# A two-layer decoder trunk on one core: sliding pooling sums rewritten as band-matrix products over tokens

## The chip, the core and the metric

The kernel runs on one core of one Trainium2 chip. The metric is the device time of one execution in microseconds (us). The core has a matrix engine (PE; its weight loads are listed apart as PEld), three engines that work on elements (DVE, ACT, POOL), and a queue engine (SP) that issues most transfers; transfers can also be issued from the queues of ACT and POOL. On-chip memory has 128 partitions; products land in eight accumulation banks of 128 x 512 values (PSUM).

## The reference, cut to what matters

The input x has 512 tokens of 1024 values. Two layers follow: layer 0 mixes tokens with a multi-scale causal pooling mixer, layer 1 with attention; after each mixer comes a SwiGLU feed-forward block (FFN), and a norm ends the trunk. The change concerns only the pooling mixer of layer 0:

```python
POOL_WINDOWS = (2, 4, 8, 16)          # one window for each group of 256 channels

def pool_mixer(h, w_in, w_group, scale, w_out):
    B, S, _ = h.shape
    u = jnp.einsum('bsd,de->bse', h, w_in).reshape(B, S, N_POOL_GROUPS, POOL_GROUP_DIM)
    cs = jnp.cumsum(u.astype(jnp.float32), axis=1)
    pos = jnp.arange(S)
    outs = []
    for g, w in enumerate(POOL_WINDOWS):
        c = cs[:, :, g]
        lag = jnp.pad(c, ((0, 0), (w, 0), (0, 0)))[:, :S]
        cnt = jnp.minimum(pos + 1, w).astype(jnp.float32)[None, :, None]
        outs.append((c - lag) / cnt - u[:, :, g].astype(jnp.float32))
    p = jnp.stack(outs, axis=2).astype(h.dtype)
    z = jnp.einsum('bsgc,gce->bsge', p, w_group).reshape(B, S, D_MODEL) * scale
    return jnp.einsum('bsd,de->bse', z, w_out)

h = rmsnorm(x, norm_mix[0]); x = x + pool_mixer(h, ...)
```

So there are three products, the input product (1024 x 1024), the group product (four times 256 x 256) and the output product (1024 x 1024), and between the first two each token's value is replaced by the mean of the last w tokens minus the value itself.

## The kernel before

**Layout.** Channels lie on partitions in eight chunks of 128 (`NC = 8`), tokens along the free side, in the order `TOKENS`: residue modulo 4 outermost (`R = 4`), 128 tokens for each residue (`J = 128`). A product of one chunk of inputs with one chunk of outputs is done in near-full precision: each operand is split into a high part and a remainder (`hi`, `lo`), and `mm3` (line 193) issues three products, of 512 columns each. A step with 8 chunks on both sides is 8 x 8 x 3 = 192 such products.

**Weights.** They are listed in use order in `queue`. `weights(i)` (line 101) loads up to five items ahead into the raw tiles of pool `wraw` (five buffers, line 63) and splits up to four ahead into pool `wspl` (three buffers, line 64): a cast on ACT makes `whi` (line 118), a subtraction on DVE makes `wlo` (line 119). All these loads are issued from SP, in order.

**What sets the order.** PE's order is written out by the program (`manual_schedule`, line 68). For the other engines the framework picks the order, one stream per engine, and a waiting instruction holds back whatever stands behind it on its engine.

**The pooling mixer before the change.** `j_two` (line 130) loads weights for outputs 0 and 1 in pieces, between the loads of x (line 334). `split_scaled` (line 312) makes `h_hi` and `h_lo` from x with the norm's gain; the squares (line 344) are added on DVE and POOL (line 347) into `norm.ssq` and `other`, and these two are added (line 348). PE starts on the input product at once: outputs 0 and 1 into two of the banks `early0` to `early3` while inputs arrive; `project` (line 198) does the others. The token norm is applied to the result: inside output 2, PE sums the squares for each token (`token_sums`, line 264, four small products), DVE and ACT take the inverse root, make four diagonal matrices (`diagonals`, line 275), and PE spreads them to all partitions (`spread`, line 285), copied to `rB`. Then for each of the eight output chunks e, in the order 6, 7, 4, 5, 2, 3, 0, 1 (line 368): `u` = result x `rB` on DVE (line 382); one to four doubling steps `winsum` on POOL and DVE (lines 391, 393, 396); `p` = sum/w - u (line 401); a correction of the first tokens (lines 406, 407); and the split into `p_hi` (ACT, line 326) and `p_lo` (POOL, line 327).

Only after all eight input products PE does the group products, in two halves of 24 products (line 410), the first on groups 3 and 2. Their results are scaled and split into `z_hi` and `z_lo` (lines 422, 423). Then come the eight output products (line 428), each followed by `residual` (line 320), which adds to x, splits for the FFN and squares for its norm. In these stages `weights` hands out `j_grp[0]`, `j_grp[1]`, `j_out[0]` to `j_out[7]`, in that order.

Of the kernel before, what the change touches and what calls it, by code (L numbers as in the profile page):

```python
# [17 lines left out]
P = 128  # L18
# [14 lines left out]
PAD = 8  # L33
# [18 lines left out]
def trunk_kernel(ctx: ExitStack, tc: tile.TileContext, xT, gam, consts, ident_d, w0, w1, wv, w_down, outT):  # L52
# [19 lines left out]

    queue = []
# [3 lines left out]
    SPLITS = {"w": 3, "v": 2}  # L77
    RAWS = {"w": 5, "v": 2}

    def enqueue(src, shape):  # L80
        queue.append(dict(kind="w", src=[src], shape=shape))
        return len(queue) - 1
# [18 lines left out]
    def weights(i, split_ahead=4, load_ahead=5):  # L101
        if "ahead" in queue[i]:
            load_ahead = queue[i]["ahead"]
        while len(raws) < min(len(queue), i + load_ahead):
            raws.append(load(queue[len(raws)]))
        while len(ready) < min(len(raws), i + split_ahead):
            item = queue[len(ready)]
            kind, shape = item["kind"], item["shape"]
            if len(ready) > i and live(ready, i, kind) == SPLITS[kind]:
                break  # L110
            n = math.prod(shape)
            raw = raws[len(ready)]
            if "plus" in item:
                nc.vector.tensor_add(raw[:, :n], raw[:, :n], raws[item["plus"]][:, :n])  # L114
            pool = pools["v"] if kind == "v" else wspl
            hi = pool.tile([P, 1024], F32R, name=kind + "hi")
            lo = pool.tile([P, 1024], F32R, name=kind + "lo")
            nc.scalar.copy(hi[:, :n], raw[:, :n])  # L118
            nc.vector.tensor_sub(lo[:, :n], raw[:, :n], hi[:, :n].bitcast(F32))  # L119
# [9 lines left out]
    PIECES = ((0, 2), (2, 2), (4, 4))  # L129
    j_two = [[enqueue(w0[i][:, s * P : (s + n) * P], (n, P)) for i in range(2)] for s, n in PIECES]  # L130
    j_in = [None, None] + [enqueue(w0[i], (8, P)) for i in range(2, 8)]
    j_grp = [enqueue(w0[8 + i], (4, 2 * P)) for i in range(2)]
    j_out = [enqueue(w0[10 + i], (8, P)) for i in range(8)]

# [58 lines left out]
    def mm3(ps, whi, wlo, xhi, xlo, first, last):  # L193
        nc.tensor.matmul(ps, lhsT=whi, rhs=xhi, start=first, stop=False)  # L194
        nc.tensor.matmul(ps, lhsT=whi, rhs=xlo, start=False, stop=False)  # L195
        nc.tensor.matmul(ps, lhsT=wlo, rhs=xhi, start=False, stop=last)  # L196
# [95 lines left out]
    class InverseRms:  # L292
# [5 lines left out]
        def columns(self):  # L298
# [4 lines left out]
            self.diag = diagonals(self.r, 4)  # L303
# [26 lines left out]
    first = []  # L330
    for (at, n), js in zip(PIECES, j_two):
        for i, w in enumerate(js):
            for c in range(at + i * n // 2, at + (i + 1) * n // 2):
                nc.sync.dma_start(x[:, c, :], xT[c * P : (c + 1) * P, :])
            first.append((at, n, i, weights(w, 1, 1)))
    nc.scalar.dma_start(ident, ident_d)
    for c in range(NC):
        split_scaled(c, 0)

    norm = Norm()  # L340
    other = tmp.tile([P, S], F32, name="rB")
    for c in range(NC):
        sq = norm.ssq if c == 0 else other if c == 1 else tmp.tile([P, S], F32, name="sq", bufs=2)
        nc.scalar.activation(sq, x[:, c, :], AF.Square)
        if c > 1:
            acc, eng = (other, nc.gpsimd) if c % 2 else (norm.ssq, nc.vector)
            eng.tensor_add(acc, acc, sq)
    nc.vector.tensor_add(norm.ssq, norm.ssq, other)

    KS = list(range(NC))  # L350
    with ExitStack() as pctx:
        pm = pctx.enter_context(tc.tile_pool(name="poolmix", bufs=1, reuse_waits="tile"))
        pw = pctx.enter_context(tc.tile_pool(name="poolw", bufs=3, reuse_waits="tile"))
        pmm = pctx.enter_context(tc.tile_pool(name="pmm", bufs=1, space=bass.MemoryType.PSUM))
        p_hi = pm.tile([P, NC, S], F32R, name="p_hi")
        p_lo = pm.tile([P, NC, S], F32R, name="p_lo")
        z_hi = pm.tile([P, NC, S], F32R, name="z_hi")
        z_lo = pm.tile([P, NC, S], F32R, name="z_lo")
        invc = pm.tile([P, 4 * R * HEAD], F32, name="invc")
        nc.scalar.dma_start(invc, consts[:, 0 : 4 * R * HEAD])  # L360
        order = [6, 7, 4, 5, 2, 3, 0, 1]


        early = [pmm.tile([P, S], F32, name=f"early{i}") for i in range(4)]
        for at, n, i, (whi, wlo) in first:
            for c in range(at, at + n):
                mm3(early[i], whi[:, c - at, :], wlo[:, c - at, :], h_hi[:, c, :], h_lo[:, c, :], c == 0, c == NC - 1)
        for n, e in enumerate(order):
            g = e // 2
            ps = early[n] if n < 4 else None  # L370
            if n == 0:
                inv_rms = InverseRms(norm.parts)
                project([j_in[2]], h_hi, h_lo, KS, early[2], {3: inv_rms.columns})
                inv_rms.rows()
                rB = inv_rms.rB
                project([j_in[3]], h_hi, h_lo, KS, early[3])
            elif n > 3:
                ps = project([j_in[n]], h_hi, h_lo, KS, ps)
            u = pw.tile([P, R, PAD + J], F32, name="u")
            nc.gpsimd.memset(u[:, :, :PAD], 0.0)  # L380
            rows = lambda t: t.rearrange("p (r j) -> p r j", r=R)
            nc.vector.tensor_mul(u[:, :, PAD:], rows(ps), rows(rB))
            s = u
            at = 0
            for lev in range(g + 1):
                sh = 1 << lev
                t = pw.tile([P, R, PAD + J], F32, name="winsum")
                eng = nc.gpsimd if lev < g - 1 or (lev == 0 and g) else nc.vector

                if sh < R:  # L390
                    eng.tensor_add(t[:, sh:, at:], s[:, sh:, at:], s[:, : R - sh, at:])
                    at += 1
                    eng.tensor_add(t[:, :sh, at:], s[:, :sh, at:], s[:, R - sh :, at - 1 : -1])
                else:
                    back = sh // R
                    eng.tensor_add(t[:, :, at + back :], s[:, :, at + back :], s[:, :, at:-back])
                    at += back
                s = t
            w = WINDOWS[g]
            p = pw.tile([P, S], F32, name="p")  # L400
            nc.vector.scalar_tensor_tensor(rows(p), s[:, :, PAD:], 1.0 / w, u[:, :, PAD:], op0=ALU.mult, op1=ALU.subtract)

            n_head = max(w // R, 1)
            hd = pw.tile([P, R, HEAD], F32, name="head")
            inv = invc[:, g * R * HEAD : (g + 1) * R * HEAD].rearrange("p (r j) -> p r j", r=R)
            nc.vector.tensor_mul(hd[:, :, :n_head], s[:, :, PAD : PAD + n_head], inv[:, :, :n_head])
            nc.vector.tensor_sub(rows(p)[:, :, :n_head], hd[:, :, :n_head], u[:, :, PAD : PAD + n_head])
            split(p_hi[:, e, :], p_lo[:, e, :], p, nc.gpsimd)
        zs = []
        for half in range(2):  # L410
            whi, wlo = weights(j_grp[half])
            for gg in range(2):
                g = 3 - (2 * half + gg)
                for m in range(2):
                    e = 2 * g + m
                    ps = early[2 * gg + m] if half == 0 else mm.tile([P, S], F32, name="mm")
# [320 lines left out]
    with ExitStack() as actx:  # L737
# [9 lines left out]
        at = 4 * R * HEAD  # L747
# [311 lines left out]
def _constants():  # L1059
    first = R * np.arange(HEAD)[None, :] + np.arange(R)[:, None]  # L1060
    inv = np.stack([np.float32(1.0) / np.minimum(first + 1, w).astype(np.float32) for w in WINDOWS])
# [13 lines left out]
    parts = [np.tile(inv.reshape(1, -1), (P, 1)), cos, sin, near, prev, near, own, comb]  # L1075
# [9 lines left out]
def _layout(x, norm_mix, norm_ffn, norm_final, pool_w_in, pool_w_group, pool_scale, pool_w_out,  # L1085
# [3 lines left out]
    w_in = _tiles(pool_w_in[0], 8)[[6, 7, 4, 5, 2, 3, 0, 1]]  # L1089
# [10 lines left out]
        xT=x[0].T[:, TOKENS], gam=gam, consts=_constants(), ident=np.eye(P, dtype=np.float32),  # L1100
# [18 lines left out]
```

## Time and profile before

| | us |
|---|---|
| median of the runs (1036.52 to 1040.21) | 1036.99 |
| the profiled execution | 1036.61 |
| its span on the core | 1034.8 |
| PE busy | 1011.8 (98% of the span) |
| DVE busy | 802.2 (78%) |
| ACT busy | 517.8 (50%) |
| POOL busy | 189.5 (18%) |
| transfers read from device memory | 140.96 MB, 138 GB/s over the span |

Times inside the profile are counted from the start of the span. A view in rows of time gives for each entry its start, its length, the engine, the line of the kernel, the operation and the tiles it writes and reads; in square brackets stands how long the engine was idle before it and what ended that. Products are pipelined in PE: a row's length includes the pipeline, so the pace is read from the distance of two starts. A product of type float32 shows as two records, the split ones (fp32r) as one. A view by stretches gives for each engine the busy time and the number of instructions in a stretch, then the granted clock of PE (1.00 is full), and the share and rate of transfers.

### The profile page before, as it was taken

The page shows a single profiled execution, that of the slowest core. Times are in us where ns is not written, and L with a number is a line of the kernel's source. Part 1 is how long each engine was busy: PE and PEld are TensorE (multiplying, and loading weights), DVE is VectorE, ACT ScalarE, POOL GpSimd, SP SyncE. Part 2 cuts the span into 40 slices and gives each one's busy share as a digit, 9 for nine tenths or more (in the row PEclk, how much of TensorE's full clock was granted, in tenths as well). Part 3 has the DMA queues.
Part 4 walks back from the last instruction along what each step waited for, and adds up shares of the span by engine and source line. Part 5 has one row for each costly group of instructions (what it writes and reads, how often), then busy time and mean ns, then how long its engine had stood idle before and what let it go on. Part 6 is the DMA issues. An engine that isn't in the chain of part 4 may idle for free.

```text
span 1034.8 us, 17396 instructions
## 1 busy us (share of the span) xinstructions
PE 1011.8 (98%) x6986; PEld 934.4 (90%) x6986; DVE 802.2 (78%) x1100; ACT 517.8 (50%) x797; POOL 189.5 (18%) x163
## 2 busy tenths in 40 slices
PE   8979999999999999999999999999999999999996
PEld 6758888999999999988777899888999999999996
DVE  6894489898888888677888636559989789788844
ACT  6243446554655555452534433444664555465444
POOL 1742300111111111022333300210011110101003
PEclk9989999999999999999999999999999999999998
DMA  7132445667668767432212143424568766966702
GB/s 271 59 102 89 141 121 135 152 194 202 163 168 233 187 139 191 141 115 82 82 45 76 52 132 94 134 82 123 123 157 216 209 149 176 230 155 163 183 29 82
DMA packets 75201, 144.19 MB, mean 139 GB/s; under 512 B 6384, under 2 KB 30576, under 8 KB 75120
## 3 DMA queue, kind: packets, MB, share of 16 engines
q1 hardware_dynamic: 56992, 113.33, 34.0%
q0 software_dynamic: 16320, 28.32, 16.9%
q10 hardware_dynamic: 1808, 1.43, 0.4%
q8 instruction: 54, 0.88, 0.3%
q14 instruction: 27, 0.22, 0.1%
HBM read 140.96 MB, written 2.10 MB: 138 GB/s over the span
## 4 chain that ended last, share of the span: by engine, by line
PE 84%; DVE 9%; issue 2%; DMA 2%; POOL 1%; ACT 1%; SPq 0%; ACTq 0%; DVEq 0%; POOLq 0%
PE p L567 29%; PE r L567 15%; PE mm L194 8%; PE mm L195 8%; PE mm L196 8%; PE mm L567 7%; DVE wlo L119 2%; PE mm L269 1%; PE mm L1008 1%; PE mm L1007 1%; PE mm L1009 1%; PE early L194 1%; PE tp L874 1%; PE early L195 1%; PE early L196 1%
## 5 line engine op out<-in xcount | busy, mean ns | idle before, releaser
L118 ACT CAST whi<-wraw 128x1024 fp32r<-128x1024 f32 (+4 forms) x201 | 194.3, 968 | 254.1 <-PE p L567 103.8
L119 DVE TENSOR_TENSOR wlo<-wraw,whi 128x1024 fp32r<-128x1024 f32 (+4 forms) x201 | 231.7, 1153 | 38.4 <-ACT whi L118 37.6
L119 DVE TENSOR_TENSOR vlo<-vraw,vhi 128x1024 fp32r<-128x1024 f32 (+1 forms) x90 | 100.3, 1116 | 42.9 <-ACT vhi L118 41.7
L118 ACT CAST vhi<-vraw 128x1024 fp32r<-128x1024 f32 (+1 forms) x90 | 86.7, 965 | 80.8 <-PE r L567 55.0
L196 PE MATMUL mm<-h_hi,wlo 128*128 128x512 f32 x312 | 121.8, 390 | 2.8 <-DVE wlo L119 2.8
L194 PE MATMUL mm<-h_hi,whi 128*128 128x512 f32 x312 | 123.7, 397 | 0.0
L195 PE MATMUL mm<-h_lo,whi 128*128 128x512 f32 x312 | 121.5, 389 | 0.0
L567 PE MATMUL p<-t_hi,whi 128*128 128x256 f32 x288 | 81.2, 282 | 0.1
L567 PE MATMUL p<-t_lo,whi 128*128 128x256 f32 x288 | 81.1, 282 | 0.0
L567 PE MATMUL r<-h_hi,vhi 128*128 128x256 f32 x288 | 81.1, 281 | 0.0
L567 PE MATMUL p<-t_hi,wlo 128*128 128x256 f32 x288 | 81.0, 281 | 0.0
L567 PE MATMUL r<-h_hi,vlo 128*128 128x256 f32 x288 | 81.0, 281 | 0.0
L567 PE MATMUL r<-h_lo,vhi 128*128 128x256 f32 x288 | 80.9, 281 | 0.0
L196 PEld LDWEIGHTS mm<-h_hi,wlo 128*128 128x128 f32 x312 | 58.6, 188 | 15.7 <-DVE wlo L119 3.2
L194 PEld LDWEIGHTS mm<-h_hi,whi 128*128 128x128 f32 x312 | 58.6, 188 | 14.1 <-issue 1.7
L195 PEld LDWEIGHTS mm<-h_lo,whi 128*128 128x128 f32 x312 | 58.6, 188 | 11.6
L114 DVE TENSOR_TENSOR vraw<-vraw,wraw 128x1024 f32<-128x1024 f32 (+1 forms) x60 | 66.9, 1115 | 0.6
L567 PE MATMUL p<-u_hi,whi 128*128 128x256 f32 x216 | 61.1, 283 | 0.0
L567 PE MATMUL p<-u_hi,wlo 128*128 128x256 f32 x216 | 61.1, 283 | 0.0
L567 PE MATMUL p<-u_lo,whi 128*128 128x256 f32 x216 | 61.0, 282 | 0.0
L98 POOL DMA_DIRECT2D wraw<-w x18 | 21.8, 1208 | 210.5 <-DVE ct L517 47.9
L250 POOL TENSOR_TENSOR ssq<-ssq,sq 128x512 f32<-128x512 f32 x20 | 32.1, 1607 | 141.7 <-issue 77.0
(278 smaller groups left out, 3004.5 us busy)
## 6 DMA issues: line engine op xcount, KB each, us to landing
wraw<-w SPq DMA_DIRECT2D x131, 512.0 KB, 3.8
wraw<-w_down SPq DMA_DIRECT2D x48, 384.0 KB, 3.3
vraw<-w SPq DMA_DIRECT2D x18, 512.0 KB, 6.1
vraw<-w POOLq DMA_DIRECT2D x18, 512.0 KB, 6.8
wraw<-w POOLq DMA_DIRECT2D x18, 512.0 KB, 7.5
vraw<-w_down SPq DMA_DIRECT2D x12, 384.0 KB, 4.1
vraw<-w_down POOLq DMA_DIRECT2D x12, 384.0 KB, 5.7
wraw<-w_down POOLq DMA_DIRECT2D x12, 384.0 KB, 6.8
```

The lines of the kernel that those rows point to most:

```text
L98: nc.gpsimd.dma_start(dst, more, accum_op=ALU.add)
L114: nc.vector.tensor_add(raw[:, :n], raw[:, :n], raws[item["plus"]][:, :n])
L118: nc.scalar.copy(hi[:, :n], raw[:, :n])
L119: nc.vector.tensor_sub(lo[:, :n], raw[:, :n], hi[:, :n].bitcast(F32))
L194: nc.tensor.matmul(ps, lhsT=whi, rhs=xhi, start=first, stop=False)
L195: nc.tensor.matmul(ps, lhsT=whi, rhs=xlo, start=False, stop=False)
L196: nc.tensor.matmul(ps, lhsT=wlo, rhs=xhi, start=False, stop=last)
L250: nc.gpsimd.tensor_add(self.ssq, self.ssq, sq)
L269: nc.tensor.matmul(cols[:, i : i + 1], lhsT=sq[:, b * P : (b + 1) * P], rhs=ones[:, :1], start=j == 0, stop=j == len(parts) - 1,)
L567: nc.tensor.matmul(ps[:, g, :], lhsT=w[:, g, c, :], rhs=xx, start=i in (0, 1, 3) and g + c + k == 0, stop=c == n - 1 and k == 2, skip_grou ...
L874: nc.tensor.transpose(tp[:, j, :], todo[i + j], ident)
L1007: nc.tensor.matmul(o, lhsT=xh, rhs=whi[:, kk, :], start=kc == 0, stop=False)
```

## The change

The tokens are put on partitions for the first half of the mixer. The roles in the input product are swapped: `h` blocks of 128 tokens are the stationary side, the weights the moving side, so a result holds 128 tokens x 512 channels. For this x is loaded in natural token order (`xN`), and a second time in the order `TOKENS` (`xT`) for the residual. The norm is then a factor for each partition, applied when a result is read out (`u_out`). The window means become products with a constant band matrix over tokens (`windows`): for each block of 128 tokens and each chunk of 128 channels, the block's `u_hi` and `u_lo` are stationary, and the band, 4 x 36 columns (the block's own tokens and up to 16 after it, for each residue), is moving; the result has channels on partitions again. Block 0 has counts below w in its band, and a third product of 16 columns for the remainder of its values. `p` is split from the bank directly (ACT and DVE).

The order on PE is new as well: first half of the input product, `token_sums` with two parts, blocks 0 and 1 of the second half, `windows(0)`, block 2, part of `windows(1)`, block 3, first group products, the rest of `windows(1)`, the known half of outputs 0 and 1, second group products, the known half of output 2, and then the output products. The second half's weights have a pool of their own (`poolb`, four buffers); when it closes, `z_hi` and `z_lo` take its place.

```diff
-    SPLITS = {"w": 3, "v": 2}
+    SPLITS = {"w": 3, "v": 2, "b": 4}
...
+    j_in = [[enqueue(w0[0][:, i * S : (i + 1) * S], (1, S)) for i in range(2)] + [enqueue(w0[i], (2, S)) for i in range(1, 4)]]
+    j_in.append([enqueue(w0[i], (2, S), "b") for i in range(4, 8)])
+    j_grp, j_out = [enqueue(w0[8], (4, 2 * P))], [enqueue(w0[10 + i], (8, P)) for i in range(2)]
+    j_grp.append(enqueue(w0[9], (4, 2 * P)))
+    j_out += [enqueue(w0[10 + i], (8, P)) for i in range(2, 8)]
...
+        held = ExitStack()
+        pools["b"] = held.enter_context(tc.tile_pool(name="poolb", bufs=4, reuse_waits="tile"))
+        early = [pmm.tile([P, S], F32, name=f"early{i}") for i in range(4)]
...
+        for c in range(NC):
+            if c < 2 or c % 2 == 0:
+                at = c if c < 2 else 1 + c // 2
+                load_x = lambda cc: nc.sync.dma_start(x[:, cc, :], xN[cc * P : (cc + 1) * P, :])
+                if c < 2:
+                    load_x(c)
+                whi, wlo = weights(j_in[0][at], 1, 1)
+                if c >= 2:
+                    load_x(c)
+                    load_x(c + 1)
+            for b in range(4):
+                blk = slice(b * P, (b + 1) * P)
+                k = 0 if c < 2 else c % 2
+                if b == 0:
+                    split_scaled(c, 0)
+                mm3(early[b], h_hi[:, c, blk], h_lo[:, c, blk], whi[:, k, :], wlo[:, k, :], c == 0, c == NC - 1)
...
+        w_second = [weights(j) for j in j_in[1]]
+        nc.sync.dma_start(bands.rearrange("p g k r j -> p (g k r j)"), consts[:, 0 : 8 * R * SPAN])
+        nc.sync.dma_start(ident, ident_d)
+        nc.scalar.copy(bands_hi, bands)
...
+        for c in range(NC):
+            nc.sync.dma_start(x[:, c, :], xT[c * P : (c + 1) * P, :])
+        inv_rms = InverseRms([norm.ssq, other])
+        inv_rms.columns(diag=False)
+
+        def u_out(b, half, ps):
+            nc.scalar.activation(u_hi[:, b, half, :], ps, AF.Copy, scale=inv_rms.r[:, b : b + 1])
+            nc.vector.scalar_tensor_tensor(
+                u_lo[:, b, half, :], ps, inv_rms.r[:, b : b + 1], u_hi[:, b, half, :].bitcast(F32),
+                op0=ALU.mult, op1=ALU.subtract,
+            )
...
+        def windows(half, blocks):
+            for i in range(4):
+                e = 4 * (1 - half) + i
+                out = early[i].rearrange("p (r j) -> p r j", r=R)
+                for b in blocks:
+                    n = min(SPAN, J - 32 * b)
+                    band = bands_hi[:, e // 2, min(b, 1), :, :n]
...
+                    mat(to, u_hi, band, start=b == 0, stop=False)
+                    mat(to, u_lo, band, start=False, stop=b == 3)
+                    if b == 0:
+                        mat(out[:, :, :HEAD], u_hi, bands_lo[:, e // 2, :, :], start=False, stop=False)
+                if blocks[-1] == 3:
+                    split(p_hi[:, e, :], p_lo[:, e, :], early[i])
...
+        for b in range(4):
+            u_out(b, 0, early[b])
+        second(0)
+        second(1)
+        windows(0, range(4))
+        second(2)
+        windows(1, range(2))
+        second(3)
+        held.close()
...
+        group_products(0, None)
+        windows(1, range(2, 4))
...
+        known, rest = [6, 7, 4, 5], [2, 3, 0, 1]
...
+        for m in range(2):
+            out_part(m, known)
+        group_products(1, early)
+        out_part(2, known)
         for m in range(NC):
-            residual(m, project([j_out[m]], z_hi, z_lo, order, early[m] if m < 4 else None), 1, norm)
+            if m > 2:
+                out_part(m, known)
+            residual(m, out_part(m, rest), 1, norm)
```

`second(b)` is the input product of token block b with the second 512 channels, 24 products into a bank of pool `mm` and then `u_out`. `out_part(m, cs)` fetches `weights(j_out[m])` at its first call and adds the chunks `cs` of output m; it keeps the split weights until its last call. The pooling loop with `winsum`, `head` and `rB`, the tiles `invc` and `u`, and the first call of `diagonals` and `spread` are gone.

More of the change, by code (lines that the diff above doesn't have):

```diff
@@ L327, in split @@
         (eng or nc.vector).tensor_sub(lo, src, hi.bitcast(F32))
[L330 to L348, printed above, removed]
     KS = list(range(NC))
     with ExitStack() as pctx:
[L352 to L354 removed]
+        open_pool = lambda name, bufs, **kw: pctx.enter_context(tc.tile_pool(name=name, bufs=bufs, reuse_waits="tile", **kw))
@@ L359, in trunk_kernel @@
[L359 to L408, printed above, removed]
@@ L409, in trunk_kernel @@
-        zs = []
-        for half in range(2):
+        u_hi = pm.tile([P, 4, 2, S], F32R, name="u_hi")
+        u_lo = pm.tile([P, 4, 2, S], F32R, name="u_lo")
+        bands = pm.tile([P, 4, 2, R, SPAN], F32, name="bands")
+        bands_hi = pm.tile([P, 4, 2, R, SPAN], F32R, name="bands_hi")
+        bands_lo = pm.tile([P, 4, R, HEAD], F32R, name="bands_lo")
+        norm = Norm()
+        other = tmp.tile([P, S], F32, name="rB")
+        for c in range(NC):
[14 more added lines that the diff above has]
+                mm3(early[b], h_hi[:, c, blk], h_lo[:, c, blk], whi[:, k, :], wlo[:, k, :], c == 0, c == NC - 1)
+            sq = norm.ssq if c == 0 else other if c == 1 else tmp.tile([P, S], F32, name="sq", bufs=2)
+            nc.scalar.activation(sq, x[:, c, :], AF.Square)
+            if c > 1:
+                acc, eng = (other, nc.gpsimd) if c % 2 else (norm.ssq, nc.vector)
+                eng.tensor_add(acc, acc, sq)
@@ new lines, in u_out, with second @@
+        def u_out(b, half, ps):
[4 more added lines that the diff above has]
+            )
+        def second(b):
+            blk = slice(b * P, (b + 1) * P)
+            ps = mm.tile([P, S], F32, name="mm")
+            for c in range(NC):
+                whi, wlo = w_second[c // 2]
+                mm3(ps, h_hi[:, c, blk], h_lo[:, c, blk], whi[:, c % 2, :], wlo[:, c % 2, :], c == 0, c == NC - 1)
+            u_out(b, 1, ps)
@@ L415, in trunk_kernel @@
                     e = 2 * g + m
-                    ps = early[2 * gg + m] if half == 0 else mm.tile([P, S], F32, name="mm")
+                    ps = banks[2 * gg + m] if banks else mm.tile([P, S], F32, name="mm")
                     for k in range(2):
@@ L1059, in _constants @@
 def _constants():
-    first = R * np.arange(HEAD)[None, :] + np.arange(R)[:, None]
-    inv = np.stack([np.float32(1.0) / np.minimum(first + 1, w).astype(np.float32) for w in WINDOWS])
+    s, d = np.arange(P)[:, None], (np.arange(R)[:, None] + R * np.arange(SPAN)[None, :]).reshape(1, -1)
+    bands = []
+    for w in WINDOWS:
+        inside = (s <= d) & (s > d - w)
+        for count in (np.minimum(d + 1, w), w):
+            bands.append(np.where(inside, np.float32(1.0) / np.float32(count), np.float32(0.0)) - (s == d).astype(np.float32))
     freq = (np.float32(1.0) / np.float32(10000.0) ** (np.arange(0, HD, 2, dtype=np.float32) / np.float32(HD))).astype(np.float32)
@@ L1074, in _constants @@
     comb = np.where((k <= q) & (k % 4 == q % 4), 0.0, NEG)
-    parts = [np.tile(inv.reshape(1, -1), (P, 1)), cos, sin, near, prev, near, own, comb]
+    parts = bands + [cos, sin, near, prev, near, own, comb]
     return np.ascontiguousarray(np.concatenate(parts, 1).astype(np.float32))
```

47 lines of the change are left out of this document (29 added, 18 removed).

## The prediction

> **What bounds the kernel now.** I read the page first: PE is busy nearly all the time, so only what PE waits for, or runs slowly, can be won.
>
> ```profile
> PE 1011.8 (98%) x6986; PEld 934.4 (90%) x6986; DVE 802.2 (78%) x1100; ACT 517.8 (50%) x797; POOL 189.5 (18%) x163
> ```
>
> Then the view by stretches, cut where PE's work changes: inputs arrive and the first products run (to 21.10), norm and outputs 2 and 3 (to 32.41), outputs 4 to 7 up to a wait (to 48.97), the rest (to 57.31), group products (to 77.18), output products (to 121.05, where the FFN's first product starts). Columns: length, busy time and count of PE, PEld, DVE, ACT, POOL, granted clock, transfer share, GB/s.
>
> ```profile
> 4.91:21.10 16.19, 15.04 (x57) 10.64 (x57) 13.09 (x19) 13.62 (x23) 4.71 (x3) 1.00 0.92 326
> 21.10:32.41 11.31, 10.94 (x57) 9.22 (x56) 7.23 (x15) 2.54 (x5) 3.00 (x4) 1.00 0.49 170
> 32.41:48.97 16.56, 16.56 (x74) 13.70 (x73) 14.87 (x22) 3.88 (x5) 12.95 (x14) 1.00 0.10 32
> 48.97:57.31 8.34, 5.51 (x24) 4.24 (x23) 8.30 (x12) 2.20 (x3) 5.90 (x6) 1.00 0.20 65
> 57.31:77.18 19.87, 14.26 (x49) 9.96 (x48) 17.92 (x28) 8.99 (x14) 7.51 (x7) 0.84 0.31 102
> 77.18:121.05 43.87, 43.87 (x194) 36.31 (x192) 20.04 (x24) 16.92 (x24) 10.73 (x6) 0.99 0.28 98
> ```
>
> The third stretch has no wait: 73 starts in 16.56 us, so a product of 512 columns costs 0.2268 us. The mixer has 192 + 48 + 192 = 432 of them, 98.0 us, and takes 121.05 - 4.91 = 116.14. The **excess is 18.2 us**. By stretch (57, 39, 73, 23, 48, 192 products): 3.3, 2.5, 0.0, 3.1, 9.0 and 0.3. The rows of PE in time show what the fourth and fifth are made of:
>
> ```profile
> 48.97 0.39 PE L195 MATMUL mm<-h_lo,whi 128*128 128x512 f32 x1
> 52.19 0.50 PE L196 MATMUL mm<-h_hi,wlo 128*128 128x512 f32 x1 [2.83 <-DVE wlo L119]
> 52.52 0.39 PE L194 MATMUL mm<-h_hi,whi 128*128 128x512 f32 x1
> 65.58 0.50 PE L196 MATMUL mm<-p_hi,wlo 128*128 128x512 f32 x1 [1.31 <-DVE wlo L119]
> 72.25 0.79 PE L194 MATMUL mm<-p_hi,whi 128*128 128x512 f32 x1 [2.62 <-ACT p_hi L326]
> 74.62 0.63 PE L194 MATMUL mm<-p_hi,whi 128*128 128x512 f32 x1
> 77.61 0.51 PE L195 MATMUL early<-z_lo,whi 128*128 128x512 f32 x1
> ```
>
> Weight remainders queue behind the pooling on DVE (busy 8.30 of 8.34 us), the last groups wait for `p`, and then seven starts take 77.61 - 74.62, 0.43 us each: half pace until 77.6.
>
> **The change part by part.** I add up what PE's excess becomes; the 432 products stay.
>
> *Pooling leaves DVE and POOL.* The groups of the span from 21 to 80 us that go (the two largest), and of three that have the form of what comes:
>
> ```profile
> L401 DVE SCALAR_TENSOR_TENSOR p<-winsum,u 128x512 f32<-128x512 f32 x8 | 7.5, 942 | 0.1
> L396 DVE TENSOR_TENSOR winsum<-winsum 128x532 f32<-128x532 f32 (+1 forms) x6 | 6.4, 1062 | 3.6 <-POOL winsum L393 3.6
> L422 ACT ACTIVATE z_hi<-mm,g_sb 128x512 fp32r<-128x512 f32 x4 | 2.6, 683 | 0.0
> L423 DVE SCALAR_TENSOR_TENSOR z_lo<-mm,g_sb,z_hi 128x512 fp32r<-128x512 f32 x4 | 2.8, 738 | 0.0
> L326 ACT CAST p_hi<-p 128x512 fp32r<-128x512 f32 x8 | 5.0, 621 | 28.2 <-DVE p L407 28.2
> ```
>
> What comes: eight `u_out` (0.68 on ACT, 0.74 on DVE) and eight splits of `p` (0.62 on ACT, about 0.7 on DVE, by the subtraction of 512 columns below), 10.4 and 11.5 us, spread over the 40 us in which PE does the second half and the groups. Neither engine is late there: the 3.1 and 9.0 us of excess go, the half pace with them.
>
> *Start.* What a chunk needs on ACT and DVE, and how the first two chunks came in before:
>
> ```profile
> 3.84 0.72 ACT L315 ACTIVATE h_hi<-x,g_sb 128x512 fp32r<-128x512 f32 x1 [1.15 <-DMA g_sb<-gam]
> 4.47 0.39 ACT L118 CAST whi<-wraw 128x256 fp32r<-128x256 f32 x1
> 6.03 0.72 ACT L315 ACTIVATE h_hi<-x,g_sb 128x512 fp32r<-128x512 f32 x1 [1.17 <-DMA x<-xT]
> 11.60 0.61 ACT L118 CAST whi<-wraw 128x512 fp32r<-128x512 f32 x1
> 12.11 0.64 ACT L344 ACTIVATE sq<-x 128x512 f32<-128x512 f32 x1
> 4.59 0.75 DVE L316 SCALAR_TENSOR_TENSOR h_lo<-x,g_sb,h_hi 128x512 fp32r<-128x512 f32 x1 [3.56 <-ACT h_hi L315]
> 12.61 0.69 DVE L119 TENSOR_TENSOR wlo<-wraw,whi 128x512 fp32r<-128x512 f32 x1
> ```
>
> Each x chunk now feeds 12 products (2.72 us) and needs 256 KB of x and 256 KB of weights, 1.6 us at the 326 GB/s of the first stretch; ACT needs 0.72 + 0.61 + 0.64 for it and DVE 0.75 + 0.69 + at most another 0.69 for the sum of squares, both under 2.72. So after the first chunk the inputs keep ahead. The first chunk's weights are 256 KB instead of 128 (0.4 us more), the cast 0.61 instead of 0.39: first product at about 5.5, the remainder of the weights at 6.2, and from there 11 products, done at 8.7. The second chunk of x came at 6.03 behind 384 KB, now behind 512: 6.4, split and ready near 8.0. Then 84 products: end at 27.8 to 28.0, an excess of **1.3 us** instead of 3.3 (from 0.5 with the old start to 3.3 if x is again late).
>
> *Norm.* The spread of `rB` goes. The token sums double, as two parts are summed: that case stands at the FFN's start, sixteen records from 123.77 to the next product at 125.47.
>
> ```profile
> 123.77 0.28 PE L269 MATMUL mm<-ones,ssq 128*128 128x1 f32 x2
> 125.47 0.49 PE L194 MATMUL mm<-h_hi,whi 128*128 128x512 f32 x1
> 627.12 0.27 PE L1036 MATMUL mm<-pT,v 128*64 128x128 f32 x1
> 627.18 0.27 PE L1038 MATMUL mm<-pT,v 128*64 128x128 f32 x1
> 300.05 0.28 PE L567 MATMUL p<-u_hi,whi 128*128 128x256 f32 x1
> 300.17 0.28 PE L567 MATMUL p<-u_lo,whi 128*128 128x256 f32 x1
> ```
>
> **1.7 us**, against 2.5. They stand right behind the first half, at 28; the last square needs x's last chunk (4.1 MB at 326 GB/s, about 15.5) and, after its split and square, one addition on POOL (4.71 us for three in the first stretch), near 20, so nothing waits. The inverse root and four `u_out` of 0.74 follow until about 34.5; blocks 0 and 1 of the second half cover them until 40.6. Without that cover it would be 5 us.
>
> *Window products.* Each half has 4 chunks x (3 + 2 + 2 + 2) = 36, together 72. No row shows this form: 144 split columns to a 128-wide stationary side. The nearest rows: with a 128-wide side even one column takes 1.70/16 = 0.106 us, 256 columns take 0.12, and with a 64-wide side 128 columns take 0.055. So the width of the stationary side sets the pace, and 144 columns lie between 0.106 and 0.12: I take 0.111, **8.0 us**. Bounds: 0.055 each, 4.0, if the loads hid as in the 64-wide rows; 16.0 if such a short split product ran as two passes like a float32 one. The sum goes by 8.0 because rows on both sides of it in columns agree.
>
> The Trainium skill, in TensorE: Matmul & The Clock Gate, section Back-to-back issue gap, gives about 81 ns for a sustained product of 128 columns with its weight load; by it the term would be an estimated 5.8 and the time 2.2 us less. Its section on weight-path perf modes excludes FP32 from fast loading, and the 0.106 us of the token sums agree with that.
>
> *New waits.* `wspl` has three buffers. When PE reaches `out_part(2)`, `j_out[0]`, `j_out[1]` and `j_grp[1]` hold them, the first two until their last calls, which come later. So the cast for `j_out[2]` can begin only when the second group products end, and PE's next product is the one that needs it. Before, a weight's cast and remainder took:
>
> ```profile
> 62.44 1.04 ACT L118 CAST whi<-wraw 128x1024 fp32r<-128x1024 f32 x1
> 56.36 1.21 DVE L119 TENSOR_TENSOR wlo<-wraw,whi 128x1024 fp32r<-128x1024 f32 x1
> ```
>
> 1.04 + 1.21 + 0.1 less two products that need no remainder (0.45): 1.9 us; 2.6 if the last `z_hi` (0.68) is ahead of it on ACT. I take **2.3**. Behind the cast on ACT stands that `z_hi`, first wanted 2.7 us later, so nobody else waits. Five more changes of step on PE with a fresh wait, about 0.1 each (after the wait at 52.19 the next start comes 0.33 later, not 0.23): **0.5**, up to 2 if a result is late.
>
> *Transfers.* SP issues in order: four second-half weights, four more items that wait for raw buffers (until about 22), then bands (590 KB), `ident` and eight x chunks (2 MB): 8 us at 326 GB/s, to about 31. Bands are wanted at 40.6, `ident` at the FFN, x at 80, and the next weights at 60. All hidden, at nothing; the old loads of `ident` and `invc` on ACT's queue go. POOL keeps three additions of squares.
>
> *Sum.* 1.3 + 1.7 + 8.0 + 2.3 + 0.5 + 0.3 (output stage as before) = 14.1 against 18.2: **4.1 us less**. Everything behind 121.05 is unchanged. The profiled execution took 1036.61 (span 1034.8 and 1.8 around it), so 1032.5; that execution lies 0.4 under the median of 1036.99, against which this is 0.43%. A measurement of this kernel can tell about 0.5%, 5.2 us, from no change: 1031.8.
>
> **The rivals.**
>
> 1. *The waits hide better.* If out 2's split finds a buffer or the start is as early as before, excess is 0.5 + 1.7 + 8.0 + 0.5 to 1 + 0.3, about 11.3: 1029.7. For it: the sums use nothing else. Against: three buffers are three. 17%.
>
> 2. *Short products take two passes*: 16.0 instead of 8.0, 1040.5, 0.35% slower. For it: float32 products show two records; against: all split products here show one, at 256, 320 and 512 columns. 12%.
>
> 3. *The clock falls in the window products*, slower than before. They fill the array for 144 columns in 0.111 us, a little over half of what 512 columns do in 0.2268. The rows show half pace here:
>
> ```profile
> 1.09 3.79 PE L230 MATMUL mm<-ones 128*128 128x128 f32 x16 [1.09 <-DVE ones L224]
> 72.00:74.00 2.00, 1.19 (x2) 0.69 (x3) 1.69 (x3) 2.00 (x4) 1.27 (x1) 0.50 0.47 193
> 633.00:640.00 7.00, 7.00 (x89) 6.49 (x86) 6.21 (x11) 2.71 (x5) 0.00 (x0) 1.00 0.07 10
> ```
>
> At the start, records with a full load take 3.79/16 = 0.237; 72 of them are 9.1 us more than at 0.111. After each of two window stretches some 12 products at 0.43, as from 72.25 to 77.6, add 2.4 each: 1032.5 + 9.1 + 4.8 = 1046.4. It decides once the clock falls inside `windows(0)`. Against it: seven microseconds of small products from 633 keep 1.00, and each window stretch is only 4 us. 6%. The Trainium skill, same page, section A second HAM failure mode: psum-queue depth-cycling, describes a clock that oscillates when PE idles briefly between groups of products; the clock of 0.50 at 72 came only behind longer waits.
>
> 4. *Read-outs arrive late*: `u_out` or `p` behind weight splits on ACT or DVE, two waits of 1.5 to 2.5: 1035 to 1037. DVE has 11.5 us of new work in 40; that speaks against. 12%.
>
> **How the numbers follow.** The forecast as summed has 53%, its own range 1030.5 to 1034.5; a third of it lies below 1031.8. Faster by over 0.5%: 0.17 + 0.17 = 0.34. Slower by over 0.5% (above 1042.2): rival 3, and rival 2 with late waits, 0.10. Within: 0.56. The range from 1029.0 to 1041.0 takes in rivals 1, 2 and 4 and leaves out rival 3 and the tails.
>
> **What would show it.** In the changed profile: the first half ends near 28 with almost no wait from 6.2 on; sixteen records of token sums in 1.7 us; window records 0.11 apart (0.22 refutes it), clock 1.00 from 5 to 115; one wait of about 2 us by a product that reads `wlo` at the start of output 2's known half; no row with `p_hi` as releaser; the FFN's first product near 117 instead of 121.05. It would be wrong if window products are not paced by loads, or if PE waits on `u_hi`, `bands_hi` or a transfer.

## The result, and the profile after

The changed kernel takes a median of 1032.68 us (five runs, 1031.56 to 1033.3), the kernel before, run beside it, 1037.83 (five runs, 1036.52 to 1040.21). The ratio is 0.9947 with a 95% interval of 0.9931 to 0.9963, so the change wins 0.53%, right at the bound of 0.5% that was set for "faster". The median forecast was 1032.5. The profiled execution took 1032.74, 3.87 less than the profiled one of before; the forecast was 4.1. The median before was 1036.99 over three runs when the forecast was made and is 1037.83 over five, so the medians lie 5.15 apart. Two more comparisons of the same kernel, further down, give ratios of 0.9933 and 0.9938.

The page of the changed kernel, its span and the busy time of each engine:

```profile
span 1030.9 us, 17461 instructions
...
PE 1016.1 (99%) x7058; PEld 943.0 (91%) x7058; DVE 783.1 (76%) x1061; ACT 522.9 (51%) x800; POOL 159.1 (15%) x131
```

PE has 4.3 us more work than before and the span is 3.9 shorter: 8.2 us in which PE did nothing are gone. Now the view by stretches, cut at each change of PE's step (columns as in the view of before: start and end, length, then busy time and count of PE, PEld, DVE, ACT, POOL, then clock, transfer share, GB/s). In order: first half of the input product, token sums, blocks 0 and 1 of the second half, `windows(0)`, block 2, part of `windows(1)`, block 3 and the first groups, the rest of `windows(1)`, known halves of outputs 0 and 1 and the second groups, the start of output 2, the outputs.

```profile
4.91:28.04 23.13, 22.20 (x97) 18.13 (x98) 21.74 (x22) 18.21 (x26) 4.66 (x3) 1.00 0.87 326
28.04:29.74 1.70, 1.70 (x18) 1.70 (x16) 0.25 (x1) 1.04 (x1) 0.00 (x0) 1.00 0.96 359
29.74:40.76 11.02, 11.02 (x50) 9.09 (x50) 5.58 (x12) 4.37 (x7) 0.00 (x0) 1.00 1.01 385
40.76:44.73 3.97, 3.97 (x38) 3.97 (x36) 2.32 (x4) 2.45 (x4) 0.00 (x0) 1.00 0.04 17
44.73:50.23 5.50, 5.50 (x26) 4.56 (x26) 1.20 (x2) 0.59 (x1) 0.00 (x0) 1.00 0.00 0
50.23:52.42 2.19, 2.19 (x21) 2.18 (x20) 0.75 (x1) 0.69 (x1) 0.00 (x0) 1.00 0.00 0
52.42:63.36 10.94, 10.94 (x50) 9.06 (x50) 2.69 (x4) 2.76 (x4) 0.00 (x0) 1.00 0.00 0
63.36:65.09 1.73, 1.73 (x17) 1.73 (x16) 0.95 (x2) 1.71 (x3) 0.00 (x0) 1.00 0.02 5
65.09:76.04 10.95, 10.95 (x50) 8.88 (x49) 5.58 (x9) 3.96 (x8) 2.54 (x2) 1.00 0.61 174
76.04:78.71 2.67, 1.24 (x5) 0.59 (x5) 1.93 (x3) 2.63 (x3) 0.00 (x0) 1.00 1.12 204
78.71:116.13 37.42, 37.42 (x167) 30.97 (x165) 20.54 (x23) 15.57 (x23) 10.04 (x6) 1.00 0.38 118
```

What to see: PE's busy time equals the length everywhere but in the first stretch and in the one at 76.04. DVE, which was busy for 8.30 of 8.34 us around PE's longest wait before, is now busy for under 60% of every stretch from 28 us on but that same one at 76.04. In the three window stretches (4, 6 and 8) PEld is busy for as long as PE: there the weight loads set the pace. PE's rows in time show the same in single products (start, length, engine, line, operation; in brackets the idle time before it and what ended it):

```profile
5.62 0.50 PE L194 MATMUL early<-whi,h_hi 128*128 128x512 f32 x1 [0.98 <-ACT whi L118]
...
40.83 0.28 PE L410 MATMUL early<-bands_hi,u_lo 128*128 128x144 f32 x1
40.94 0.22 PE L410 MATMUL early<-bands_lo,u_hi 128*128 128x16 f32 x1
41.01 0.32 PE L410 MATMUL early<-bands_hi,u_hi 128*128 128x144 f32 x1
41.16 0.28 PE L410 MATMUL early<-bands_hi,u_lo 128*128 128x144 f32 x1
41.27 0.27 PE L410 MATMUL early<-bands_hi,u_hi 128*128 128x144 f32 x1
41.38 0.28 PE L410 MATMUL early<-bands_hi,u_lo 128*128 128x144 f32 x1
...
77.11 0.50 PE L194 MATMUL mm<-z_hi,whi 128*128 128x512 f32 x1 [0.91 <-ACT whi L118]
77.45 0.40 PE L195 MATMUL mm<-z_lo,whi 128*128 128x512 f32 x1
78.37 0.50 PE L196 MATMUL mm<-z_hi,wlo 128*128 128x512 f32 x1 [0.52 <-DVE wlo L119]
...
116.13 0.39 PE L194 MATMUL mm<-h_hi,whi 128*128 128x512 f32 x1
```

The window products start 0.11 us apart on average. The one of 16 columns and the next one take 0.22 together (40.94 to 41.16), as two of 144 columns do (41.16 to 41.38): the number of columns makes no difference here. Output 2 waits first for the cast of its weights and then for their remainder. The FFN starts at 116.13 instead of 121.05.

That is 4.92 us, and the span is 3.9 shorter. The table follows the lead of the changed kernel over the one before, at the same product of the FFN and of layer 1 in both profiles, counted in records from the FFN's first:

| record | before | after | lead |
|---|---|---|---|
| FFN's first product | 121.05 | 116.13 | 4.92 |
| the 312th after it | 180.0 | 173.85 | 6.16 |
| first token sum before attention's first product | 465.2 | 458.95 | 6.25 |
| 39 records later | 471.9 | 468.81 | 3.09 |
| the last record | 1027.87 | 1024.44 | 3.43 |

So behind the mixer there are two more differences: the FFN's start gains 1.24, and attention's start loses 3.16. Here are PE's rows at attention's start, of the kernel before and then of the changed one:

```profile
466.11 0.38 PE L269 MATMUL mm<-ones,sq 128*128 128x1 f32 x2 [0.41 <-ACT sq L246]
...
467.92 0.58 PE L269 MATMUL mm<-ones,sq 128*128 128x1 f32 x4
468.36 0.48 PE L194 MATMUL mm<-h_hi,whi 128*128 128x512 f32 x1
468.68 0.39 PE L195 MATMUL mm<-h_lo,whi 128*128 128x512 f32 x1
```

```profile
459.86 0.38 PE L269 MATMUL mm<-ones,sq 128*128 128x1 f32 x2 [0.41 <-ACT sq L246]
...
461.70 0.99 PE L269 MATMUL mm<-ones,sq 128*128 128x1 f32 x4
462.56 0.77 PE L194 MATMUL mm<-h_hi,whi 128*128 128x512 f32 x1
463.13 0.63 PE L195 MATMUL mm<-h_lo,whi 128*128 128x512 f32 x1
...
467.82 0.63 PE L194 MATMUL mm<-h_hi,whi 128*128 128x512 f32 x1
```

The instructions and the wait of 0.41 are the same in both, but the changed kernel slows down within its last token sums (0.99 for four instead of 0.58), and from 462.56 on its products start 0.43 us apart (the first two 0.57), for 13 products. The view by stretches has a granted clock of 0.50 there, and 0.87 over the token sums ahead of it, in which PE was busy for 3.20 of 3.61 us:

```profile
458.95:462.56 3.61, 3.20 (x26) 3.11 (x24) 1.57 (x2) 2.14 (x3) 0.00 (x0) 0.87 0.47 147
462.56:468.25 5.69, 5.69 (x14) 4.44 (x15) 3.06 (x10) 1.94 (x4) 0.00 (x0) 0.50 0.05 18
```

### The profile page after: what moved, and what is told of

It is laid out like the page before. It is cut to its first block, busy times and chain, and to the rows that moved or that the text cites. A ratio compares the mean times of both kernels' runs of the same rounds, so it can differ in the third digit from the quotient of the medians.

```text
span 1030.9 us, 17461 instructions
## 1 busy us (share of the span) xinstructions
PE 1016.1 (99%) x7058; PEld 943.0 (91%) x7058; DVE 783.1 (76%) x1061; ACT 522.9 (51%) x800; POOL 159.1 (15%) x131
## 4 chain that ended last, share of the span: by engine, by line
PE 95%; DVE 2%; ACT 1%; issue 0%; DMA 0%; POOL 0%; ACTq 0%; DVEq 0%; POOLq 0%
PE p L607 30%; PE r L607 15%; PE mm L194 11%; PE mm L196 11%; PE mm L195 10%; PE mm L607 8%; PE mm L269 1%; PE mm L1048 1%; PE mm L1047 1%; PE early L195 1%; PE mm L1049 1%; PE early L194 1%; PE early L196 1%; PE tp L914 1%; PE early L410 1%; DVE h_lo L317 1%
## 5 line engine op out<-in xcount | busy, mean ns | idle before, releaser
L118 ACT CAST whi<-wraw 128x1024 fp32r<-128x1024 f32 (+3 forms) x194 | 189.7, 979 | 257.9 <-PE p L607 103.1
L119 DVE TENSOR_TENSOR wlo<-wraw,whi 128x1024 fp32r<-128x1024 f32 (+3 forms) x194 | 225.7, 1163 | 38.4 <-ACT whi L118 37.5
L194 PE MATMUL mm<-h_hi,whi 128*128 128x512 f32 x280 | 112.5, 402 | 0.0
L196 PE MATMUL mm<-h_hi,wlo 128*128 128x512 f32 x280 | 110.2, 393 | 0.0
L195 PE MATMUL mm<-h_lo,whi 128*128 128x512 f32 x280 | 110.1, 393 | 0.0
L194 PEld LDWEIGHTS mm<-h_hi,whi 128*128 128x128 f32 x280 | 53.3, 190 | 13.1 <-issue 1.7
L196 PEld LDWEIGHTS mm<-h_hi,wlo 128*128 128x128 f32 x280 | 53.2, 190 | 11.6
L195 PEld LDWEIGHTS mm<-h_lo,whi 128*128 128x128 f32 x280 | 53.3, 190 | 10.5
L607 PEld LDWEIGHTS p<-t_hi,whi 128*128 128x128 f32 x288 | 54.3, 189 | 0.0
```

Source lines behind the costliest of these rows:

```text
L607: nc.tensor.matmul(ps[:, g, :], lhsT=w[:, g, c, :], rhs=xx, start=i in (0, 1, 3) and g + c + k == 0, stop=c == n - 1 and k == 2, skip_grou ...
```

## The experiments

The theory: pooling on DVE and POOL had cost PE about 12 us; as products it costs PE 8 us, paced by weight loads, and one wait at output 2 that the new order itself makes. What was open: whether the interleaved order is worth that wait; where the FFN's 1.24 came from; whether half pace at attention belongs to the change.

### The changed kernel again, with output 2 moved, and in a plain order

The first run is the changed kernel once more.

> The changed kernel again, for the stretch around 462 us, where its profile shows 13 products at half pace (0.43 us) and loses 2.7 us. Theory 'chance of the clock': the mixer again ends with the FFN's first product at 116.1 (within 0.2), but the half pace may be absent, and then the span is about 1028 to 1029. Rival 'it belongs to the changed kernel': half pace again at 462 and a span of 1030.9.

Median 1032.59 (1030.56 to 1033.42), ratio 0.9933, 0.9908 to 0.9958. Its profile differs at the two places where half pace was seen: the first products run at half pace, and the FFN starts 1.30 later, at 117.43; attention's start loses 1.6 instead of 3.2 (40 records that take 6.93 in the profile of before take 8.52 here and took 10.09 in the first profile of the changed kernel). Its rows at the start:

```profile
5.44 0.80 PE L194 MATMUL early<-whi,h_hi 128*128 128x512 f32 x1 [0.56 <-ACT whi L118]
...
7.18 0.63 PE L194 MATMUL early<-whi,h_hi 128*128 128x512 f32 x1
7.61 0.63 PE L195 MATMUL early<-wlo,h_hi 128*128 128x512 f32 x1
```

Starts 0.43 apart, while the stretches have a granted clock of 1.00 from 7 to 9 us: at the start, that column doesn't show it. Two profiles of the same kernel differ by 1.3 us at the first place and by 1.6 at the second, so the runs below are read at their steps and not by their spans.

The second run gives up the known half of output 2 ahead of the loop:

```diff
-        out_part(2, known)
...
-            if m > 2:
+            if m > 1:
```

> Output 2's known half moves from before output 0's end to just before its own end, so that at no time three split weights are held. Theory 'three buffers make the wait': the two waits of 0.91 and 0.52 us at 77.1 and 78.4 go with their restarts, the FFN starts 2.0 us earlier, at 114.1. Rival 'the wait moves': output 0's remaining half then waits for the last z_lo (ready near 77.5 with the work queued on DVE), 0.5 to 1.5 us, and the FFN starts at 114.6 to 116.

```profile
78.96 0.50 PE L195 MATMUL mm<-z_lo,whi 128*128 128x512 f32 x1 [0.57 <-DVE z_lo L431]
```

The FFN starts at 114.91, 1.22 earlier than in the changed kernel; the median is 1030.4 (1028.66 to 1030.57), ratio 0.9906 (0.9877 to 0.9934), an interval that overlaps the one of the run just above. The wait for output 2's weights is gone, and the row above takes part of its place. DVE's rows tell why: output 2's remainder still stands ahead of the last `z_lo`.

```profile
77.02 1.22 DVE L119 TENSOR_TENSOR wlo<-wraw,whi 128x1024 fp32r<-128x1024 f32 x1 [0.74 <-ACT whi L118]
78.16 0.74 DVE L431 SCALAR_TENSOR_TENSOR z_lo<-early,g_sb,z_hi 128x512 fp32r<-128x512 f32 x1
```

So a stretch with 2.0 us in excess becomes one wait of 0.57 and its restart. The wait for output 2's weights came with the order of the steps on PE; what is left comes from the order on DVE, in which a weight split that is wanted later stands ahead of a result that is wanted now.

The third run takes all interleaving out: the whole input product, both halves of the windows, both group products, then the outputs one by one.

```diff
         second(0)
         second(1)
+        second(2)
+        second(3)
         windows(0, range(4))
-        second(2)
-        windows(1, range(2))
-        second(3)
+        windows(1, range(4))
...
-        windows(1, range(2, 4))
+        group_products(1, early)
...
-        for m in range(2):
+        for m in range(NC):
             out_part(m, known)
-        group_products(1, early)
-        out_part(2, known)
-        for m in range(NC):
-            if m > 2:
-                out_part(m, known)
             residual(m, out_part(m, rest), 1, norm)
```

The queue is put in the matching order, both `j_grp` and then the eight `j_out`.

> The window products stay, the interleaving goes: the whole input product, windows of both halves, both group products, then the output products one by one. Theory 'the gain is the leaving of DVE and POOL, not the order': windows of one half cover the read-out of the other, the group products of the first half cover the last p, no weights are held over; FFN at 114.1 to 114.5, as without the wait for output 2. Rival 'the interleaving hides read-outs': waits with p_lo, u_lo or z_lo as releaser of 1.5 us each at two or three places, FFN at 117 to 119.

PE's waits between 5 and 117 us in this kernel (line waited for, total, times, longest):

```profile
PE early L193 <- ACT whi L118: 0.6, 1, 0.6
```

That is the first product's; from there to the FFN PE waits for nothing. The FFN starts at 115.48 although this profile has half pace at the start (its first half ends at 29.43 instead of 28.04); without these 1.39 it would be near 114.1, 2.0 before the changed kernel, as long as output 2's wait. Median 1030.25 (1027.88 to 1030.63), ratio 0.9903 (0.9874 to 0.9933). The interleaved order hides nothing that the plain one doesn't hide, and costs that wait.

### Each window product twice

```diff
                     mat(to, u_hi, band, start=b == 0, stop=False)
+                    mat(to, u_hi, band, start=False, stop=False)
+                    mat(to, u_lo, band, start=False, stop=False)
                     mat(to, u_lo, band, start=False, stop=b == 3)
```

The product with `bands_lo` is issued twice as well, so the pooled values are doubled.

> Every window product is issued twice (the pooled values come out doubled). Theory 'paced by the weight load': 72 more at 0.110, 7.9 us more, FFN at 124.0, time 8 us above the changed kernel. Rival 'paced by columns, the load hidden': repeats of the same stationary block cost 144/512 of 0.2268 or less, 0.06 each, 4.5 us or less. Rival 'clock': small products in a stretch of 8 us pull the granted clock to 0.5, more than 12 us.

The FFN starts at 124.12, 7.99 later than in the changed kernel: 72 more products cost 0.111 each, although the second of a pair has the same stationary side as the one directly before it. Median 1042.39 (1038.16 to 1044.11), ratio to before 1.0017 (0.9996 to 1.0037). PEld shows the bound in the view by stretches; PE and PEld are both busy without a gap:

```profile
40.76:44.73 3.97, 3.97 (x38) 3.97 (x37) 1.44 (x2) 1.27 (x2) 0.00 (x0) 1.00 0.24 93
```

### The kernel before without its pooling, and with its tiles in another order

The first of these has no window sums and no correction of the first tokens, `p = u`; everything else is the kernel before.

```diff
-            nc.vector.tensor_mul(u[:, :, PAD:], rows(ps), rows(rB))
...
+            nc.vector.tensor_mul(p, ps, rB)
```

> The kernel before without the window sums: p is u itself, so the doubling steps, the difference and the correction of the first tokens are left out; the rest is as before. Theory 'the pooling on DVE and POOL made the excess of 3.1 and 9.0 us': the waits at 52.2 and 63.5 go, at the end a wait of about 2 us for the last p stays (POOL's p_lo takes 1.5), half pace goes; the FFN starts at 110.5 to 112, 9 to 10 us less. Rival 'the order of the stages made it' (all group products behind all input products): waits of 5 us or more stay there, less than 5 us won.

The FFN starts at 108.52, 12.53 earlier than in the kernel before: pooling had cost PE 12.5 us, where the prediction read 3.1 + 9.0 out of its two stretches. Median 1026.41 (1024.85 to 1027.33), ratio 0.9874 (0.9847 to 0.99). The waits of PE from 5 to 109 us that are left:

```profile
PE early L195 <- DVE h_lo L316: 0.6, 2, 0.3
PE mm L269 <- DVE ssq L348: 0.4, 1, 0.4
PE early L194 <- ACT h_hi L315: 0.3, 1, 0.3
PE early L196 <- DVE wlo L119: 0.2, 1, 0.2
```

None is at a group or output product. The FFN's first 312 records take 59.14 here, 58.96 in the kernel before and 57.72 in the changed kernel and all its variants above, so a mixer with less work for DVE and POOL is not what speeds up the FFN's start.

The other tries a different cause for that gain. SP issues the FFN's first load of its `v` weights at 121.24 before and at 66.13 after:

```profile
121.24 1.07 SPq L96 DMA_DIRECT2D vraw<-w  x2
```

```profile
66.13 0.90 SPq L96 DMA_DIRECT2D vraw<-w  x2
```

The idea was that the tile it writes takes memory that another tile of the mixer has to leave first. So in the kernel before, `z_hi` and `z_lo` were placed ahead of `p_hi` and `p_lo`.

> The kernel before with one edit: z_hi and z_lo are placed ahead of p_hi and p_lo, so that the FFN's first accumulated weight tile lies over p, free after the group products at 77, and not over z, free after the output products at 121. Theory 'early tile': its load is issued near 77 instead of 121, and the FFN's first 312 records take 57.7 us as in the changed kernel instead of 59.0; 1.2 us less in all. Rival 'it comes from elsewhere in the change' (less work on DVE or POOL): 59.0 us as before.

The load came at 119.07, not at 77, so the run doesn't test an early load. Median 1038.79 (1035.77 to 1041.5), ratio 0.9999 (0.9983 to 1.0015). Its first 312 records take 58.20, 0.76 less than before, without an early load; where these 0.76 come from is seen in the last experiment.

### The start with more idle products, and the best order

Behind the profiled starts stood the suspicion that PE's idle gap before its first product (0.98 us in the changed kernel, 0.56 in its second run) brings on half pace there. `range(8)` became `range(10)` in the loop of idle products at the kernel's start, and the changed kernel ran beside it once more.

> The changed kernel once more beside the two others. By chance of the clock the start (13 products at half pace cost 1.3 us) and the beginning of the attention (up to 3.2 us) differ from profile to profile; the mixer without them takes the same 111 us. If the half pace belongs to one place of the program, the two earlier profiles agree with this one.

> The changed kernel with ten idle products instead of eight ahead of the first real one, and nothing else. Theory 'the later first product opens a gap in which the clock may start low': the start is at full pace, the FFN near 116.1, and the median lies 0.5 to 1.3 below the changed kernel's on the same chip, since the slow start costs 1.3 us in a part of the executions. Rival 'chance, whatever the gap': no difference above 0.3.

With ten: 1031.55 (1030.07 to 1035.0), ratio 0.9927 (0.9902 to 0.9951). With eight: 1033.04 (1031.5 to 1035.46), ratio 0.9938 (0.9916 to 0.996). The medians lie 1.49 apart, but the intervals overlap. Both profiles start at full pace, with the FFN at 116.11 and 115.97. Of eight profiles of the changed family with eight idle products, those of the last experiment included, three start at half pace, of two with ten none does; that is too few to tell whether the two more products help. The gap as a cause finds no support: the three slow starts have the shortest gaps of the eight, 0.56 to 0.59 us, the five at full pace 0.61 to 1.15.

Two runs collect what is worth having. Both use the plain order and add the two parts of the sum of squares on DVE, so that PE sums one part for each token instead of two; the second of them has ten idle products too.

```diff
-        inv_rms = InverseRms([norm.ssq, other])
+        nc.vector.tensor_add(norm.ssq, norm.ssq, other)
+        inv_rms = InverseRms(norm.parts)
```

> The changed kernel in the plain order of the earlier run, and the squares added on DVE into one part, so that the token sums are eight records instead of sixteen. Theory: 0.89 us less on PE than the plain order, the addition of 0.7 us on DVE lies near 20 us and is hidden: FFN at 113.3 with a full-pace start (114.5 with a slow one), median about 1029.3. Rival 'the addition is late': PE waits at the token sums with ssq as releaser, nothing is won.

> As the last, with ten instead of eight idle products ahead of the first real one, to fill the gap of PE from 4.6 to 5.5 us. Theory 'the gap lets the clock start low in some executions': no half pace at 6 to 9 us, the FFN at 113.3 to 113.6, and the times spread less; median 0.3 to 0.8 below the last kernel. Rival 'chance alone, the clock has a window of its own': half pace may still show there, and the median does not move by more than 0.3; if the ten run past 5.5 they cost up to 0.5 us.

Rows of the first of them:

```profile
28.04 0.95 PE L268 MATMUL mm<-ones,ssq 128*128 128x1 f32 x8
28.85 0.49 PE L193 MATMUL mm<-bhi,h_hi 128*128 128x512 f32 x1
...
113.21 0.39 PE L193 MATMUL mm<-h_hi,whi 128*128 128x512 f32 x1
```

Token sums take 0.81 us instead of 1.70, and nobody waits for the addition. The FFN starts at 113.21, and at 113.06 in the second: 2.92 and 3.07 before the changed kernel. The medians are 1031.77 (1027.06 to 1033.64), ratio 0.9917 (0.9895 to 0.994), and 1028.28 (1026.95 to 1031.52), ratio 0.9895 (0.9875 to 0.9915). The second has the lowest ratio of the complete kernels. Its interval lies below two of the changed kernel's three (0.9931 to 0.9963 and 0.9916 to 0.996) and overlaps the third (0.9908 to 0.9958). Neither is told apart from the plain order (0.9874 to 0.9933) by these runs: what they win is seen at the steps, not in the medians.

### The changed kernel with a late load of `v`

`p_hi` and `p_lo` get a pool of their own ahead of `u` and the bands, which go to the other end of memory.

```diff
+        p_hi = pm.tile([P, NC, S], F32R, name="p_hi")
+        p_lo = pm.tile([P, NC, S], F32R, name="p_lo")
...
-        p_hi = pm.tile([P, NC, S], F32R, name="p_hi")
-        p_lo = pm.tile([P, NC, S], F32R, name="p_lo")
+        pm = open_pool("poolu", 1, side="right")
```

> The changed kernel with the tiles of u and the bands moved to the other end of the on-chip memory, so that the FFN's first accumulated weight tile lies over z instead of u. Theory 'early tile': its load is issued near 116 instead of 66, the FFN's first 312 records take 59.0 us again instead of 57.7, the mixer still ends at 116.1; 1.2 us more. Rival 'less work on DVE and POOL makes the FFN's start faster': 57.7 us stay.

```profile
117.92 0.90 SPq L96 DMA_DIRECT2D vraw<-w  x2
```

The load is late now, and the first 312 records take 58.21, 0.49 more than in the changed kernel; 59.0 had been expected if the load were the whole cause. So 0.5 of the 1.24 goes with the early load. Median 1034.37 (1030.58 to 1035.18), ratio 0.9949 (0.993 to 0.9967).

Most of the other 0.75 lies at one product of the FFN, where the lead of the changed kernel grows from 4.92 to 5.49. In the kernel before, this product waits for DVE:

```profile
168.01 0.39 PE L567 MATMUL p<-h_lo,whi 128*128 128x256 f32 x1 [0.41 <-DVE h_lo L327]
```

Neither the changed kernel nor the two runs with other places have this wait; the kernel without pooling has it too (0.59). The rows of ACT and DVE lead from it back to the same `v` weights:

```profile
132.30 1.05 ACT L118 CAST vhi<-vraw 128x1024 fp32r<-128x1024 f32 x1 [2.94 <-DMA vraw<-w]
133.39 1.22 DVE L119 TENSOR_TENSOR vlo<-vraw,vhi 128x1024 fp32r<-128x1024 f32 x1 [2.77 <-ACT vhi L118]
167.25 2.44 DVE L327 TENSOR_TENSOR h_lo<-hn,h_hi 128x512 fp32r<-128x512 f32 x3
```

The cast waits for the transfer, the remainder for the cast, and from the remainder at 133.39 on DVE works without a gap up to the `h_lo` that PE wants. Counted from the FFN's first product, that remainder begins at 12.53 in the kernel without pooling (wait 0.59), at 12.34 in the kernel before (0.41), and at 11.60 in both runs with other places (no wait). So this part, too, goes with the time at which the first `v` weights arrive. Why they arrive 0.74 sooner in the last run, whose load is issued 0.19 behind the FFN's first product as in the kernel before, is open.

## Why the prediction was right

The measured excess over 432 products at 0.2268 us, from the stretches above, against the terms of the sum:

| step | forecast | measured |
|---|---|---|
| start, first half | 1.3 | 1.36 (23.13 less 96 x 0.2268) |
| token sums | 1.7 | 1.70 |
| window products | 8.0 | 7.89 (3.97 + 2.19 + 1.73) |
| output 2's wait | 2.3 | 1.99 (2.67 less 3 x 0.2268) |
| changes of step | 0.5 | 0.30 |
| output stage | 0.3 | 0.00 (37.42 is 165 x 0.2268) |
| sum | 14.1 | 13.2 |

**Pooling leaves DVE and POOL: right.** No row has `p_hi` as releaser, and the kernel without pooling puts what goes at 12.5 us, against the forecast's 12.1.

**Start and norm: right.** The first half ends at 28.04. A start at half pace, 1.3 us more, was in no term, and three profiles of eight show it.

**Window products: right, and shown twice**, by the stretches and by the doubled products: 0.110 and 0.111 us. Two passes are out, as each product is one record. The Trainium skill, in TensorE: Matmul & The Clock Gate, section Back-to-back issue gap, gives 81 ns for a product of 128 columns; for these split float32 products the trace doesn't agree, and its 0.110 decides.

**Output 2's wait: right in cause, 0.3 too long.** The cast begins when the second group products end, as said, and two rows carry the wait, 0.91 and 0.52. The last `z_hi` stood behind it on ACT, as taken. The rival that this wait finds cover is out for the order as it was written; the plain order, which the forecast did not weigh, has no such wait.

**The clock in the window products: the rival is out there.** The clock is 1.00 from 5 to 115, as the forecast asked, even with the windows doubled, and the pace of 0.11 says the same. The half pace that the rival meant came somewhere else, at attention's start.

**"Everything behind 121.05 is unchanged": wrong, in both directions.** This is the step that failed. The mixer gained 4.92 instead of 4.1; the FFN's start gained 1.24 more, of which 0.5 goes with the load of `v` weights that the new tile places let start 55 us sooner, and most of the rest with a wait in the kernel before that hangs on the same weights; and half pace at attention's start, in this execution and not in the profiled one of before, took back 3.16. With these, and 0.4 in small differences elsewhere, the lead at the last record is 3.43, and the spans differ by 3.9. That the total came out 0.2 us from the forecast is luck in good part, since these errors cancel: with both profiles at full pace there the lead at the last record would have been about 6.6 us (3.43 + 3.16).

The prediction's chances had 0.56 on "within 0.5%" and 0.34 on "faster"; the ratio of 0.9947 lies just on the "faster" side, with an interval (0.9931 to 0.9963) that reaches to both.

## What to carry to other kernels

A chain of element operations can be moved to the matrix engine as many small products if that engine waited longer for the chain than the small products cost: count them by the weight-load pace of a row with the same stationary width, which held here from 1 to 144 columns. Before interleaving steps by hand, look at whether the plain order waits at all; here it didn't, and each step that was pulled ahead held a weight buffer that the next one wanted. And a change of tiles in one stage moves when the next stage's loads are issued, so the places behind the change are compared too, product by product.

## What the runs showed of the hardware

Half pace came in some executions and not in others, behind the same instructions. At attention's start, with a wait of 0.41 us within 3.2 to 3.6 us of single-column products, the same 40 records took 6.90 to 6.93 us in the profile of before and in four others, 8.48 to 8.52 in six, and 10.09 in two: steps of 1.6 us. Kernels of both families are among the slower ones (two variants of before at 8.48 and 8.50), so it is not the change alone that brings it, and the window products, 4 us of 0.11 each and 8 when doubled, never did. The Trainium skill, in the same page, section What's actually happening, describes a clock of two rates that falls after an idle window of about 3.4 us, windows that run freely. The two paces, 0.2268 and 0.43, agree with two rates; but PE was idle there for only 0.41 us, in one piece. What decides in one execution and not in the next, no run here shows.

The column of the granted clock had 0.50 for the half pace at 462 us and 1.00 for the same pace at 7 us, so at the start the distance of two starts is the better reading. The column isn't blind there in every profile: in the kernel before with its tiles in another order it has 0.50 from 8 to 11 us.
